# Two accumulators per bank or one: the PSUM placement of a seven-product matrix stage

## The chip, the cores and the metric

The kernel runs on one core of one Trainium2 chip. The metric is the device time of one execution in microseconds (us), lower being better. Before the change it is 1694.95 us, the median of three runs (1694.61 to 1696.0).

## What is computed

A two-layer encoder trunk over 512 tokens of width 1024. Each layer adds a mixer of three attention branches to its input, then a feed-forward block. The change touches one product inside the second of these, the down projection:

```python
def conv_ffn(h, w_up, conv_w, conv_b, w_down):        # h: (1, 512, 1024)
    u = h @ w_up                                      # w_up: (1024, 5632)
    u = depthwise_conv3(u, conv_w) + conv_b
    a, g = jnp.split(u, 2, axis=-1)
    return (jax.nn.gelu(g) * a) @ w_down              # w_down: (2816, 1024)

for l in range(2):
    x = x + mixer(rmsnorm(x, norm1_g[l]))
    x = x + conv_ffn(rmsnorm(x, norm2_g[l]), w_up[l], conv_w[l], conv_b[l], w_down[l])
```

All of it is float32, and the kernel keeps more precision than one float32r pass of TensorE has: every operand is split into a high part (rounded to float32r) and a low part (the rest), and a product is three matmuls, high by high, high by low and low by high.

## The kernel before

**Layout.** Activations lie transposed: `self.x[k]` is block k of 128 features by 512 tokens, k from 0 to 7. A weight block of 128 by 128 is the stationary operand, and 512 (or 256) token columns move past it. PSUM has eight banks of 512 float32 columns per partition, and `bank("d")` hands them out in turn, here as a ring of eight.

**The seven-product stage.** Of the 22 blocks of 128 hidden features, the first 12 go through a Strassen-like scheme instead of a plain product. The tokens are cut in two halves of 256, the hidden blocks into even and odd ones, and the output blocks are taken in pairs (m, m+1), for m = 0, 2, 4, 6. For such a pair, which this text calls a unit, eight block products are replaced by seven products of sums, each of 6 stationary blocks with 3 matmuls, so 18 matmuls of 256 columns. A stage has 4 units, 28 products and 504 matmuls, and there is one stage per layer, placed among the up projections as soon as the first 12 hidden blocks are there; up projections (`("up", f)`, matmuls of 512 columns) stand before and after it.

The moving operands (the tiles `ft`, columns B11, T1, B21, T2, B22, T4, T3) are made once, in `sum_operands`. The stationary operands are sums of the down weights, made per unit by `prepare_sum` (L165 to L180): four pieces come by DMA (tiles `own` and `raw`), VectorE adds them up to S1 (L169), S3 (L173), S2 (L174) and S4 (L177), and `split` (L192 and L193) makes of each a high part `whi` on ScalarE and then a low part `wlo` on VectorE. There are three buffers for a `whi` and `wlo` pair, so the pair for product j+3 can be written once product j has been multiplied.

**The accumulators.** In a unit the products, numbered j = 0 to 6, go into PSUM regions that are summed further where the scheme wants running sums. After every product VectorE adds the region, or subtracts it, into a half of `x[m]` or `x[m+1]` (L1010, 256 columns; for j = 6 into both halves, L1013). This read is called an eviction below. The region isn't cleared afterwards: a later product in the same region adds to what stands there, and is read out again. Before the change the four regions are the two halves of two banks:

- bank 0, first half: j = 0, 3 and 6; second half: j = 2
- bank 1, first half: j = 1 and 4; second half: j = 5

The first matmul into a bank carries the start flag (`start=j < 2 and i == 0`). [...]

**Order.** PE and the DMA queue of SP run in the order of the code. ScalarE and VectorE are ordered by a list scheduler, in which evictions have a higher priority (`high_priority(offset=EVAC)`). The framework puts the semaphore waits in, and it treats a bank as one thing: a matmul into a bank waits until VectorE's earlier reads of that bank are over, whichever half they read.

Of the kernel before, what the change touches and what calls it, by code (L numbers as in the profile page):

```python
# [41 lines left out]
B11, B21, B22, T1, T3, T2, T4 = range(7)  # L42
# [20 lines left out]
class Trunk:  # L63
# [926 lines left out]
    def do_sum(self, m):  # L990


        nc, mm = self.nc, self.nc.tensor.matmul
        banks = [self.bank("d") for _ in range(2)]
        first, second = slice(0, 256), slice(256, 512)
        x1, x2 = self.x[m], self.x[m + 1]
        steps = ((B11, 0, first, x1[:, first], 1), (T1, 1, first, x2[:, second], -1), (B21, 0, second, x1[:, first], 1),
                 (T2, 0, first, x1[:, second], 1), (B22, 1, first, x1[:, second], 1), (T4, 1, second, x2[:, first], -1),
                 (T3, 0, first, x2, -1))
        for j, (spec, (operand, b, part, x, sign)) in enumerate(zip(self.W["sum", m], steps)):  # L1000
            ps = banks[b][:, part]
            c = slice(operand * 256, operand * 256 + 256)
            for i, (wh, wl) in enumerate(self.weights(spec)):
                hi, lo = (t[:, c] for t in self.ff[i])
                mm(ps, wh, hi, start=j < 2 and i == 0, stop=False, skip_group_check=True)  # L1005
                mm(ps, wh, lo, start=False, stop=False, skip_group_check=True)  # L1006
                mm(ps, wl, hi, start=False, stop=i == NP - 1, skip_group_check=True)  # L1007
            with self.tc.high_priority(offset=EVAC):
                if j < 6:
                    nc.vector.tensor_tensor(x, x, ps, ALU.add if sign > 0 else ALU.subtract)  # L1010
                else:
                    both = x.rearrange("p (n c) -> p n c", c=256)
                    nc.vector.tensor_tensor(both, both, ps.rearrange("p (n c) -> p n c", n=1).to_broadcast([P, 2, 256]),  # L1013
                                            ALU.subtract)
        if m == KD - 2:
            self.ff = self.ff[NP:]
            self.fas.close()
            self.fbs, self.fb = self.open("fb")
# [202 lines left out]
```

## Time and profile before

| What | Value |
|---|---|
| Three timed runs | 1694.95 us median, 1694.61 to 1696.0 |
| The profiled execution, its own time | 1695.11 us |
| Its span in the profile | 1693.3 us |
| Instructions | 23333 |
| TensorE (PE) busy | 1673.5 us, 99% |
| Weight loads (PEld), beside PE | 1402.3 us, 83% |
| VectorE (DVE) busy | 1216.9 us, 72% |
| ScalarE (ACT) busy | 867.7 us, 51% |
| DMA engines, mean | 92 GB/s |

How to read the profile: busy time counts each engine's instructions in one profiled execution. A PE row in the timeline has its start, its modelled length, and in brackets the idle time before it with the instruction that ended this. Matmuls overlap: one of 256 columns is shown 0.28 us long, and the next begins well before it ends. So PE's pace is read from the distance between starts, not from lengths. Where a row waited for several semaphores, the profile names the one it takes to have come last.

### The profile page before, as it was taken

The page shows a single profiled execution, that of the slowest core. Times are in us where ns is not written, and L with a number is a line of the kernel's source. Part 1 is how long each engine was busy: PE and PEld are TensorE (multiplying, and loading weights), DVE is VectorE, ACT ScalarE, POOL GpSimd, SP SyncE. Part 2 cuts the span into 40 slices and gives each one's busy share as a digit, 9 for nine tenths or more (in the row PEclk, how much of TensorE's full clock was granted, in tenths as well). Part 3 has the DMA queues.
Part 4 walks back from the last instruction along what each step waited for, and adds up shares of the span by engine and source line. Part 5 has one row for each costly group of instructions (what it writes and reads, how often), then busy time and mean ns, then how long its engine had stood idle before and what let it go on. Part 6 is the DMA issues. An engine that isn't in the chain of part 4 may idle for free.

```text
span 1693.3 us, 23333 instructions
## 1 busy us (share of the span) xinstructions
PE 1673.5 (99%) x8898; PEld 1402.3 (83%) x8898; DVE 1216.9 (72%) x2033; ACT 867.7 (51%) x1525; POOL 52.1 (3%) x107
## 2 busy tenths in 40 slices
PE   9999999999999999999999999999999999999998
PEld 8888888888888888888887888888888888888887
DVE  7677866787559897676567687767866598876755
ACT  7664445775435443344466554567744454433443
POOL 1110000000000000000011100000000000000000
PEclk9999999999999999999999999999999999999999
DMA  6233323222333333432232323332233333323322
GB/s 181 71 97 91 88 79 88 77 65 80 111 87 112 99 83 92 125 99 76 83 96 81 96 77 93 82 87 69 63 87 105 103 111 101 90 73 113 93 81 88
DMA packets 289664, 155.53 MB, mean 92 GB/s; under 512 B 9136, under 2 KB 285632, under 8 KB 289552
## 3 DMA queue, kind: packets, MB, share of 16 engines
q1 hardware_dynamic: 287008, 148.88, 30.9%
q0 software_dynamic: 2256, 4.83, 0.9%
q8 instruction: 70, 1.15, 0.3%
q14 instruction: 42, 0.34, 0.1%
q10 hardware_dynamic: 288, 0.33, 0.1%
HBM read 151.89 MB, written 2.10 MB: 91 GB/s over the span
## 4 chain that ended last, share of the span: by engine, by line
PE 94%; DVE 4%; ACT 1%; issue 0%; DMA 0%; ACTq 0%
PE ps_ring L206 12%; PE ps_ring L207 12%; PE ps_ring L208 12%; PE ps_d L208 10%; PE ps_d L206 10%; PE ps_d L207 10%; PE ps_g L206 4%; PE ps_g L208 4%; PE ps_g L207 4%; PE ps_d L1005 2%; PE ps_d L1006 2%; PE ps_d L1007 2%; PE ps_ring L286 2%; PE ps_ring L273 1%; DVE wlo L193 1%; PE ps_g L306 1%
## 5 line engine op out<-in xcount | busy, mean ns | idle before, releaser
L192 ACT CAST whi<-raw 128x1024 fp32r<-128x1024 f32 (+3 forms) x347 | 297.3, 857 | 508.6 <-PE ps_ring L207 152.5
L193 DVE TENSOR_TENSOR wlo<-raw,whi 128x1024 fp32r<-128x1024 f32 (+4 forms) x345 | 339.2, 983 | 83.2 <-ACT whi L192 82.5
L208 PE MATMUL ps_d<-hh,wlo 128*128 128x512 f32 x685 | 266.6, 389 | 0.0
L207 PE MATMUL ps_d<-hl,whi 128*128 128x512 f32 x685 | 266.5, 389 | 0.0
L206 PE MATMUL ps_d<-hh,whi 128*128 128x512 f32 x685 | 266.5, 389 | 0.0
L206 PE MATMUL ps_ring<-hh,whi 128*128 128x512 f32 x600 | 235.3, 392 | 0.5 <-DVE pt L717 0.5
L208 PE MATMUL ps_ring<-hh,wlo 128*128 128x512 f32 x600 | 233.7, 390 | 0.0
L207 PE MATMUL ps_ring<-hl,whi 128*128 128x512 f32 x600 | 233.6, 389 | 0.0
L208 PEld LDWEIGHTS ps_d<-hh,wlo 128*128 128x128 f32 x685 | 128.6, 188 | 27.1 <-DVE wlo L193 0.2
L207 PEld LDWEIGHTS ps_d<-hl,whi 128*128 128x128 f32 x685 | 128.6, 188 | 26.9
L206 PEld LDWEIGHTS ps_d<-hh,whi 128*128 128x128 f32 x685 | 128.6, 188 | 26.3
L206 PEld LDWEIGHTS ps_ring<-hh,whi 128*128 128x128 f32 x600 | 112.6, 188 | 24.5 <-DVE pt L717 0.9
L208 PEld LDWEIGHTS ps_ring<-hh,wlo 128*128 128x128 f32 x600 | 112.6, 188 | 23.7
L207 PEld LDWEIGHTS ps_ring<-hl,whi 128*128 128x128 f32 x600 | 112.7, 188 | 23.0
L1005 PE MATMUL ps_d<-ft,whi 128*128 128x256 f32 x336 | 96.4, 287 | 10.9 <-DVE x L1010 8.1
L1006 PE MATMUL ps_d<-ft,whi 128*128 128x256 f32 x336 | 95.0, 283 | 0.0
L1007 PE MATMUL ps_d<-ft,wlo 128*128 128x256 f32 x336 | 94.9, 283 | 0.0
L199 DVE TENSOR_TENSOR u<-ps_d,rb 128x512 f32<-128x512 f32 x80 | 55.1, 689 | 54.3 <-PE ps_d L208 54.0
L199 DVE TENSOR_TENSOR gz<-ps_ring,rb 128x512 f32<-128x512 f32 x44 | 30.4, 691 | 78.0 <-PE ps_ring L208 78.0
L1005 PEld LDWEIGHTS ps_d<-ft,whi 128*128 128x128 f32 x336 | 64.2, 191 | 14.1 <-issue 9.0
L193 DVE TENSOR_TENSOR pl<-ps_ring,ph 128x512 fp32r<-128x512 f32 x104 | 65.6, 682 | 1.6 <-ACT ph L192 1.6
L1006 PEld LDWEIGHTS ps_d<-ft,whi 128*128 128x128 f32 x336 | 64.4, 192 | 0.1
(355 smaller groups left out, 3262.9 us busy)
## 6 DMA issues: line engine op xcount, KB each, us to landing
raw<-in_w_in_dram SPq DMA_DIRECT2D x86, 512.0 KB, 3.9
raw<-in_w_up_dram SPq DMA_DIRECT2D x80, 512.0 KB, 3.8
raw<-in_w_down_dram SPq DMA_DIRECT2D x32, 384.0 KB, 3.6
own<-in_w_down_dram SPq DMA_DIRECT2D x16, 384.0 KB, 4.9
raw<-in_w_in_dram SPq DMA_DIRECT2D x17, 256.0 KB, 3.0
raw<-in_w_br_mla_dram SPq DMA_DIRECT2D x16, 256.0 KB, 2.8
raw<-in_w_br_na_dram SPq DMA_DIRECT2D x16, 256.0 KB, 2.9
raw<-in_w_br_gqa_dram SPq DMA_DIRECT2D x16, 256.0 KB, 2.9
```

Source lines behind the costliest of these rows:

```text
L192: nc.scalar.copy(hi, src)
L193: nc.vector.tensor_sub(lo, src, r32(hi))
L199: self.nc.vector.tensor_tensor(out, a, b, ALU.mult)
L206: mm(ps, sh, mh, start=first and k == 0, stop=False)
L207: mm(ps, sh, ml, start=False, stop=False)
L208: mm(ps, sl, mh, start=False, stop=last and k == n - 1)
L273: self.nc.tensor.transpose(out[i][:, n * 64:n * 64 + 64], block[q], self.idf[q, q])
L286: self.nc.tensor.matmul(out, st[a], mv[b], start=first and t == 0, stop=last and t == 2)
L306: self.nc.tensor.matmul(self.gbank[j], w[:, j * P:(j + 1) * P], m, start=n + t == 0, stop=False)
L1005: mm(ps, wh, hi, start=j < 2 and i == 0, stop=False, skip_group_check=True)
L1006: mm(ps, wh, lo, start=False, stop=False, skip_group_check=True)
L1007: mm(ps, wl, hi, start=False, stop=i == NP - 1, skip_group_check=True)
```

## The change

Each unit takes four banks in place of two, and uses the first 256 columns of each. B11, T2 and T3 (j = 0, 3, 6) stay together in the first, T1 and B22 (j = 1, 4) in the second; B21 (j = 2) has the third for itself and T4 (j = 5) the fourth. Four matmuls per unit carry the start flag in place of two. The number of matmuls, their operands and the evictions' arithmetic are the same. A stage takes 16 turns of the ring of eight in place of 8, so the banks that are handed out after it are the same as before.

```diff
-        banks = [self.bank("d") for _ in range(2)]
+        banks = [self.bank("d")[:, :256] for _ in range(4)]
...
-        steps = ((B11, 0, first, x1[:, first], 1), (T1, 1, first, x2[:, second], -1), (B21, 0, second, x1[:, first], 1),
-                 (T2, 0, first, x1[:, second], 1), (B22, 1, first, x1[:, second], 1), (T4, 1, second, x2[:, first], -1),
-                 (T3, 0, first, x2, -1))
-        for j, (spec, (operand, b, part, x, sign)) in enumerate(zip(self.W["sum", m], steps)):
-            ps = banks[b][:, part]
+        steps = ((B11, 0, x1[:, first], 1), (T1, 1, x2[:, second], -1), (B21, 2, x1[:, first], 1),
+                 (T2, 0, x1[:, second], 1), (B22, 1, x1[:, second], 1), (T4, 3, x2[:, first], -1), (T3, 0, x2, -1))
+        for j, (spec, (operand, b, x, sign)) in enumerate(zip(self.W["sum", m], steps)):
+            ps, fresh = banks[b], j in (0, 1, 2, 5)
...
-                mm(ps, wh, hi, start=j < 2 and i == 0, stop=False, skip_group_check=True)
+                mm(ps, wh, hi, start=fresh and i == 0, stop=False, skip_group_check=True)
```

The function is one line shorter, so L1005, L1006, L1007, L1010 and L1013 of before are L1004, L1005, L1006, L1009 and L1012 of the changed kernel.

The first place is on PE, in the first unit of the first stage, where j = 2 (B21) ends and j = 3 (T2) begins; `ps_d` is the accumulator's bank tile, and a bracket names the engines whose semaphores the row waits for. Before:

```order
L1005 MATMUL ps_d_6083<-ft_5903,whi_6085 128x256
L1006 MATMUL ps_d_6083<-ft_5904,whi_6085 128x256
L1007 MATMUL ps_d_6083<-ft_5903,wlo_6086 128x256
L1005 MATMUL ps_d_6083<-ft_5089,whi_6115 128x256 [waits DVE_49,Activation_49]
L1006 MATMUL ps_d_6083<-ft_5090,whi_6115 128x256
L1007 MATMUL ps_d_6083<-ft_5089,wlo_6116 128x256
```

And in the changed kernel:

```order
L1004 MATMUL ps_d_6085<-ft_5903,whi_6087 128x256
L1005 MATMUL ps_d_6085<-ft_5904,whi_6087 128x256
L1006 MATMUL ps_d_6085<-ft_5903,wlo_6088 128x256
L1004 MATMUL ps_d_6083<-ft_5089,whi_6117 128x256 [waits DVE_49,Activation_49]
L1005 MATMUL ps_d_6083<-ft_5090,whi_6117 128x256
L1006 MATMUL ps_d_6083<-ft_5089,wlo_6118 128x256 [waits DVE_49]
```

Nothing moved, but the tiles differ: before, j = 2 and j = 3 write the same bank tile (6083); now j = 2 has a tile of its own (6085), and j = 3 goes back to the tile of j = 0.

The second place is on PE too, in the same unit, where j = 4 (B22) ends and j = 5 (T4) begins. Before:

```order
L1005 MATMUL ps_d_6084<-ft_5903,whi_6138 128x256
L1006 MATMUL ps_d_6084<-ft_5904,whi_6138 128x256
L1007 MATMUL ps_d_6084<-ft_5903,wlo_6139 128x256
L1005 MATMUL ps_d_6084<-ft_5089,whi_6161 128x256 [waits DVE_49,Activation_49]
L1006 MATMUL ps_d_6084<-ft_5090,whi_6161 128x256
L1007 MATMUL ps_d_6084<-ft_5089,wlo_6162 128x256
```

And in the changed kernel:

```order
L1004 MATMUL ps_d_6084<-ft_5903,whi_6140 128x256
L1005 MATMUL ps_d_6084<-ft_5904,whi_6140 128x256
L1006 MATMUL ps_d_6084<-ft_5903,wlo_6141 128x256
L1004 MATMUL ps_d_6086<-ft_5089,whi_6163 128x256 [waits Activation_49]
L1005 MATMUL ps_d_6086<-ft_5090,whi_6163 128x256
L1006 MATMUL ps_d_6086<-ft_5089,wlo_6164 128x256 [waits DVE_49]
```

The first matmul of j = 5 has a new tile and no longer waits for VectorE; the third, which reads `wlo`, does. In all, the double wait (VectorE and ScalarE) stands on j = 2, 3 and 5 of a unit before, and on j = 3, 4 and 6 now, 24 of them in two stages either way.

The third place is on VectorE, in the second unit of the first stage; `x2_69` and `x3_70` are the outputs into which its evictions add, `wlo` rows are low parts of weights, L169, L173 and L177 the weight sums. Before, from the eviction of the unit ahead (j = 6) on:

```order
L169 TENSOR_TENSOR s1_6385<-raw_6287,own_6289 128x768 [waits DMAHW5_49,DMAHW4_49,DVE_49]
L1013 TENSOR_TENSOR x1_68<-x1_68,ps_d_6083 128x512 [waits PE_49]
L193 TENSOR_TENSOR wlo_6262<-raw_6234,whi_6261 128x768 [waits DMAHW2_49,Activation_49]
L173 TENSOR_TENSOR raw_6287<-own_6285,raw_6287 128x768 [waits DMAHW3_49,DVE_49]
L1010 TENSOR_TENSOR x2_69<-x2_69,ps_d_6259 128x256 [waits PE_49]
L177 TENSOR_TENSOR raw_6234<-own_6109,raw_6234 128x768 [waits DVE_49]
L193 TENSOR_TENSOR wlo_6292<-own_6109,whi_6291 128x768 [waits Activation_49]
L1010 TENSOR_TENSOR x3_70<-x3_70,ps_d_6260 128x256 [waits PE_49]
L193 TENSOR_TENSOR wlo_6315<-raw_6234,whi_6314 128x768 [waits Activation_49]
L1010 TENSOR_TENSOR x2_69<-x2_69,ps_d_6259 128x256 [waits PE_49]
L193 TENSOR_TENSOR wlo_6338<-own_6113,whi_6337 128x768 [waits Activation_49]
```

And in the changed kernel:

```order
L1012 TENSOR_TENSOR x1_68<-x1_68,ps_d_6083 128x512 [waits DVE_49,PE_49]
L169 TENSOR_TENSOR s1_6389<-raw_6291,own_6293 128x768 [waits DMAHW5_49,DMAHW4_49,DVE_49]
L193 TENSOR_TENSOR wlo_6266<-raw_6236,whi_6265 128x768 [waits DMAHW2_49,Activation_49]
L1009 TENSOR_TENSOR x2_69<-x2_69,ps_d_6261 128x256 [waits PE_49]
L173 TENSOR_TENSOR raw_6291<-own_6289,raw_6291 128x768 [waits DMAHW3_49,DVE_49]
L193 TENSOR_TENSOR wlo_6296<-own_6111,whi_6295 128x768 [waits Activation_49]
L177 TENSOR_TENSOR raw_6236<-own_6111,raw_6236 128x768 [waits DVE_49]
L1009 TENSOR_TENSOR x3_70<-x3_70,ps_d_6262 128x256 [waits PE_49]
L1009 TENSOR_TENSOR x2_69<-x2_69,ps_d_6263 128x256 [waits DVE_49,PE_49]
L193 TENSOR_TENSOR wlo_6319<-raw_6236,whi_6318 128x768 [waits Activation_49]
L193 TENSOR_TENSOR wlo_6342<-own_6115,whi_6341 128x768 [waits Activation_49]
```

The weight sum L169, which waits for a DMA, now stands behind the eviction of j = 6; the eviction of j = 2 (the second `x2_69` row) now stands ahead of the low part for j = 4 (`wlo_6319`), and was behind it. Outside the stages VectorE, ScalarE, PE and SP keep their order.

## The prediction

> **What bounds the kernel now.** I read the page first, then PE's waits, then the timeline of PE and VectorE through one stage. Of the page:
>
> ```profile
> span 1693.3 us, 23333 instructions
> PE 1673.5 (99%) x8898; PEld 1402.3 (83%) x8898; DVE 1216.9 (72%) x2033; ACT 867.7 (51%) x1525; POOL 52.1 (3%) x107
> PE 94%; DVE 4%; ACT 1%; issue 0%; DMA 0%; ACTq 0%
> L1005 PE MATMUL ps_d<-ft,whi 128*128 128x256 f32 x336 | 96.4, 287 | 10.9 <-DVE x L1010 8.1
> ```
>
> PE is the bound, and the chain that ends last runs through it for 94%. So only what shortens PE's own stream, or its gaps, counts. The last row is the one big gap on the page: before the first kind of seven-product matmul PE stands idle for 10.9 us. PE's waits, longest first in total, say for whom:
>
> ```profile
> PE ps_d L1005 <- DVE x L1010: 8.1, 13, 0.7
> PE ps_d L1005 <- ACT whi L192: 2.6, 3, 0.9
> ```
>
> Sixteen waits: two in each of the eight units. The timeline of the third unit of the first stage shows both kinds (columns: start, length, engine and line; in brackets the idle time ahead and what ended it).
>
> ```profile
> 653.75 0.28 PE L1006 MATMUL ps_d<-ft,whi 128*128 128x256 f32 x1
> ...
> 664.30 0.28 PE L1007 MATMUL ps_d<-ft,wlo 128*128 128x256 f32 x1
> 665.18 0.36 PE L1005 MATMUL ps_d<-ft,whi 128*128 128x256 f32 x1 [0.61 <-DVE x L1010]
> 665.37 0.28 PE L1006 MATMUL ps_d<-ft,whi 128*128 128x256 f32 x1
> ...
> 670.34 0.36 PE L1005 MATMUL ps_d<-ft,whi 128*128 128x256 f32 x1 [0.61 <-DVE x L1010]
> ```
>
> ```profile
> 664.61 0.42 DVE L1010 TENSOR_TENSOR x<-x,ps_d 128x256 f32<-128x256 f32 x1 [0.18 <-PE ps_d L1007]
> ```
>
> The first is the start of j = 3, the second of j = 5. Each goes into the bank that the product just ended has filled the other half of (j = 2, j = 4). So PE ends at 664.30 + 0.28 = 664.58, VectorE reads from 664.61 to 665.03, and PE goes on 0.15 later, at 665.18. The loss isn't the 0.61 of the bracket. Between gaps matmuls start (664.30 - 653.75) / 88 = 0.1199 apart (88 steps between those two rows). The gap is 0.88 from start to start, so 0.76 is lost, and another 0.07 at the second matmul (0.19 in place of 0.12): 0.83 per wait.
>
> The three waits put down to ScalarE are of the same kind, with VectorE late. In the second unit:
>
> ```profile
> 646.97 0.95 DVE L193 TENSOR_TENSOR wlo<-raw,whi 128x768 fp32r<-128x768 f32 x1
> 647.84 0.42 DVE L1010 TENSOR_TENSOR x<-x,ps_d 128x256 f32<-128x256 f32 x1
> ```
>
> ```profile
> 648.40 0.35 PE L1005 MATMUL ps_d<-ft,whi 128*128 128x256 f32 x1 [0.89 <-ACT whi L192]
> ```
>
> The row of PE comes 0.14 after the eviction's end (647.84 + 0.42), as above; the eviction had a low part of weights ahead of it (one such takes VectorE 0.87 until the next can start).
>
> **The size of it.** I don't add up sixteen rows, but take the length of the two stages, from the first matmul of 256 columns to the first up projection behind:
>
> ```profile
> 623.82 0.28 PE L1005 MATMUL ps_d<-ft,whi 128*128 128x256 f32 x1
> ...
> 691.50 0.40 PE L206 MATMUL ps_d<-hh,whi 128*128 128x512 f32 x1
> ```
>
> ```profile
> 1461.73 0.28 PE L1005 MATMUL ps_d<-ft,whi 128*128 128x256 f32 x1
> ...
> 1530.02 0.40 PE L206 MATMUL ps_d<-hh,whi 128*128 128x512 f32 x1
> ```
>
> 67.68 and 68.29 us; 504 matmuls at 0.1199 are 60.43. So 7.25 + 7.86 = 15.1 us are lost in the two stages. That is the most that taking every wait out can give. Sixteen times 0.83 is 13.3; the rest is the late evictions and three short waits at j = 2.
>
> **The change, part by part.**
>
> *The waits at j = 3 and j = 5.* The order's rows show j = 5 going into a bank of its own without a wait for VectorE ahead of its first matmul, and j = 3 returning to the bank of j = 0, two products earlier. The same holds for j = 4 (bank of j = 1) and j = 6 (bank of j = 3). Two products are 36 × 0.1199 = 4.3 us for an eviction that needs 0.03 + 0.42 + 0.15 = 0.6, so it may queue 3.7 us on VectorE before PE notices. The short waits at j = 2 go as well. Term: -15.1.
>
> *The double waits.* There are 24 of them as before, now all on evictions long over. What one costs then, the row of j = 2 in the second unit shows, whose eviction had ended 0.2 earlier:
>
> ```profile
> 645.20 0.29 PE L1005 MATMUL ps_d<-ft,whi 128*128 128x256 f32 x1
> 645.33 0.28 PE L1006 MATMUL ps_d<-ft,whi 128*128 128x256 f32 x1
> ```
>
> 0.13 to the next in place of 0.12. Term: 24 × 0.01 = +0.24; between nothing and 0.07 each (1.7), the restart after a real wait.
>
> *Start flags.* Two more per unit on matmuls that run anyway: the rows of 623.82 (with) and 653.75 (without) are alike, 0.28. Nothing; the sum goes unchanged with it.
>
> *What is late next.* Weights. In the first unit of each stage VectorE is still busy with the convolution:
>
> ```profile
> 631.71 0.95 DVE L193 TENSOR_TENSOR wlo<-raw,whi 128x768 fp32r<-128x768 f32 x1
> ```
>
> ```profile
> 628.22 0.36 PE L1005 MATMUL ps_d<-ft,whi 128*128 128x256 f32 x1
> ```
>
> That `wlo` is for j = 4 and its queue ahead is unchanged, so it ends at 632.66, and PE can use it 0.15 later, at 632.81. Undelayed, j = 2 starts at 628.13 (the row's 628.22 less its wait of 0.09), and the third matmul of j = 4 is 38 steps on, at 632.69. So about 0.12 + 0.07 = 0.2 stays, once per stage: +0.4.
>
> In the second unit VectorE now evicts j = 2 before it makes the low part for j = 4, and its queue is held up first by a DMA. The worst case is in the second stage:
>
> ```profile
> 1473.78 0.54 SPq L163 DMA_DIRECT2D own<-in_w_down_dram  x1
> ```
>
> ```profile
> 641.36 0.96 DVE L169 TENSOR_TENSOR s<-raw,own 128x768 f32<-128x768 f32 x1 [0.68 <-DMA own<-in_w_down_dram]
> ...
> 1471.36 0.70 DVE L199 TENSOR_TENSOR c<-c 128x512 f32<-128x512 f32 x1
> ...
> 1479.61 0.96 DVE L169 TENSOR_TENSOR s<-raw,own 128x768 f32<-128x768 f32 x1 [1.01 <-DMA own<-in_w_down_dram]
> ```
>
> ```profile
> 664.54 0.83 ACT L192 CAST whi<-own 128x768 fp32r<-128x768 f32 x1 [1.23 <-PE ps_d L1006]
> ```
>
> The sum (last VectorE row) waited for a DMA that was issued 5.8 us earlier, and SP had issued that once a low part on VectorE, for j = 6 of the unit ahead, had freed a buffer. In the changed order this low part no longer has L199 in front of it, 0.7, so the sum starts at about 1478.9. The unit starts on PE at 1461.73 + 126 × 0.1199 + 0.2 = 1477.0, so the sum comes 1.9 us into it. Behind it stand in turn a low part (0.87), an eviction (0.4), a sum (0.87), the low part for j = 3, which ends at about 5.8 and is needed at 56 × 0.1199 = 6.7; then a sum until 6.7, two evictions, the second of which can't start before j = 2 is over (6.6), until 7.3; meanwhile the high part of j = 4 on ScalarE, 0.83, until 7.6; and its low part until 8.6. PE needs that at 74 × 0.1199 = 8.87, less 0.15. It fits by 0.1; in the first stage, where the same sum came 17.54 after the stage's start (641.36) and not 17.88, by 0.4. I take zero, with 0.5 for the range. VectorE as a whole has room:
>
> ```profile
> 641.00:691.60 50.60, 37.11 (x51) 1.00 0.28 80
> ```
>
> 37.11 us of work in three units, where the shorter stage leaves 3 × 15.1 = 45.3.
>
> *The sum.* -15.1 + 0.24 + 0.4 = -14.5 us. Nothing behind the stage takes it back: the up projections that follow have their banks in the same turn, and PE runs through them without idle time. The span of 1693.3 becomes 1678.8, the profiled execution's own 1695.11 becomes 1680.6, and the median of 1694.95, which is 0.16 lower, 1680.5.
>
> **The clock, and a rule for the pace.** PE's granted clock through the stages, and ahead of them (window, its length, busy time and count of PE, PEld, DVE, ACT and POOL, then the clock, DMA share and GB/s):
>
> ```profile
> 580.00:623.80 43.80, 43.80 (x195) 36.27 (x194) 37.46 (x54) 19.93 (x28) 0.00 (x0) 1.00 0.37 102
> 623.80:691.50 67.70, 62.44 (x505) 60.92 (x504) 52.85 (x76) 26.05 (x32) 0.72 (x1) 1.00 0.30 83
> ```
>
> Full clock with gaps and without. The pace of 0.1199 for 256 columns could itself come from two accumulators sharing a bank. The up projections, with whole banks, tell against it:
>
> ```profile
> 619.74 0.39 PE L206 MATMUL ps_d<-hh,whi 128*128 128x512 f32 x1
> ...
> 623.59 0.39 PE L208 MATMUL ps_d<-hh,wlo 128*128 128x512 f32 x1
> ```
>
> 17 steps in 3.85 us are 0.2265 for 512 columns, so 0.1066 for each 256 columns more, and 0.013 per matmul whatever its length. The overhead is there in whole banks too, so the pace stays. [...]
>
> **Rivals.**
>
> *Weights take over* (0.12). VectorE or the DMA is later than walked through, and PE waits for `wlo` where it waited for the bank. For it: margins of 0.1 to 0.4 in four units. Against: 3 us of slack per unit. At 0.5 to 1.5 us in each of the eight units 4 to 12 of the 14.5 are lost; likelier the low end: 1682.5 to 1688.
>
> *Half of it* (0.03). The rows give the engine that j = 3 waits for, not which instruction of it. Were it still the eviction just ahead, only the waits at j = 5 would go, 8 × 0.83 = 6.6: 1688.3. The bank tile speaks against it.
>
> *Nothing* (0.03). Every bank wait turns into a weight wait of its length: 1695.
>
> *The pace* (0.01). The share of the bank does slow the matmuls; by the difference at 512 columns no more than 0.013 each, 1008 × 0.013 = 13 us more: 1667.5.
>
> *Slower* (0.03). [...]
>
> **How the numbers follow.** My forecast, 0.78, is 1680.5, its own range 1679.3 (all 15.1, and 0.5 for the spread of the runs) to 1683 (the double waits at 0.07, the 0.5 of the margins, and the spread again). For 8 in 10 the range goes on into the first rival's near half: 1679 to 1685. About 0.2% (3.4 us) is what a measurement of this kernel tells from no change. Faster by more: 0.78 + 0.12 + 0.03 + 0.01 = 0.94; within: 0.03; slower: 0.03.
>
> **What would show it.** The stages should take about 60.7 us each, PE's idle time ahead of the first matmul line of the stage should fall from 10.9 us to under 1, and the waits for the eviction should leave PE's list. VectorE's evictions then end later relative to PE without anybody waiting. A new row in which PE waits for `wlo` (L193), of 0.1 to 0.2 us once per stage, is expected; such rows in every unit would be the first rival. [...] If the stages shrink by 14 us and the whole doesn't, I was wrong about what stands behind them.

## The result and the profile after

| | Before | After |
|---|---|---|
| Median | 1695.18 us (four runs, 1694.61 to 1696.0) | 1682.05 us (four runs, 1681.14 to 1682.36) |
| Ratio, with its 95% interval | | 0.9921 [0.9904, 0.9938] |
| Profiled execution: own time, span | 1695.11, 1693.3 us | 1681.14, 1679.3 us |
| First stage, from its first matmul to the first up projection behind | 67.68 us | 60.92 us |
| Second stage | 68.29 us | 61.47 us |

The change makes the kernel 13.1 us faster (a fourth run of the kernel before has moved its median from 1694.95 to 1695.18). The forecast was 1680.5, and the range reached from 1679 to 1685. The last two rows of the table come from these rows of PE's timeline after the change:

```profile
623.24 0.28 PE L1004 MATMUL ps_d<-ft,whi 128*128 128x256 f32 x1
...
684.16 0.40 PE L206 MATMUL ps_d<-hh,whi 128*128 128x512 f32 x1
...
1454.56 0.28 PE L1004 MATMUL ps_d<-ft,whi 128*128 128x256 f32 x1
...
1516.03 0.40 PE L206 MATMUL ps_d<-hh,whi 128*128 128x512 f32 x1
```

The stages are 6.76 and 6.82 us shorter, 13.6 in all. The stretch between them is the same (770.40 us, 770.23 before), and so is the one behind them (1679.3 - 1516.03 = 163.27, and 1693.3 - 1530.02 = 163.28 before): what was gained in a stage was kept. The remaining 0.4 of the 14.0 between the two spans comes from the stretch ahead of the first stage, which began at 623.24 in place of 623.82; the change touches nothing there. Runs of one kernel differ by that much: in a second profile of the changed kernel the first stage begins at 623.72.

The page after the change, in the lines that answer to those of before:

```profile
span 1679.3 us, 23339 instructions
PE 1669.9 (99%) x8898; PEld 1400.5 (83%) x8898; DVE 1214.5 (72%) x2033; ACT 866.9 (52%) x1525; POOL 52.6 (3%) x107
L1006 PE MATMUL ps_d<-ft,wlo 128*128 128x256 f32 x336 | 95.6, 284 | 0.5 <-DVE wlo L193 0.4
L1004 PE MATMUL ps_d<-ft,whi 128*128 128x256 f32 x336 | 95.1, 283 | 0.0
```

PE's idle time ahead of the first of the three matmul lines fell from 10.9 us to 0.0. In its place the third one, which reads the low part of the weights, shows 0.5. In the list of PE's waits the eviction (L1009) doesn't stand any more, and the one row on the stage is:

```profile
PE ps_d L1006 <- DVE wlo L193: 0.4, 1, 0.4
```

What an eviction does now can be seen where j = 4 ends in the third unit of the first stage. VectorE reads the bank from 664.92 on, while PE goes on with j = 5 in another bank at its pace of 0.12:

```profile
664.92 0.42 DVE L1009 TENSOR_TENSOR x<-x,ps_d 128x256 f32<-128x256 f32 x1 [0.45 <-PE ps_d L1006]
```

```profile
664.96 0.28 PE L1006 MATMUL ps_d<-ft,wlo 128*128 128x256 f32 x1
665.08 0.28 PE L1004 MATMUL ps_d<-ft,whi 128*128 128x256 f32 x1
```

**What is left.** 504 matmuls at 0.1199 are 60.43 us, so 0.5 and 1.0 us are still lost. The largest single loss is in the second stage, at j = 3 of the third unit:

```profile
1491.74 0.28 PE L1005 MATMUL ps_d<-ft,whi 128*128 128x256 f32 x1
1492.41 0.39 PE L1006 MATMUL ps_d<-ft,wlo 128*128 128x256 f32 x1 [0.40 <-DVE wlo L193]
1492.63 0.28 PE L1004 MATMUL ps_d<-ft,whi 128*128 128x256 f32 x1
```

0.67 and 0.22 from start to start in place of 0.12 each: 0.65 lost. VectorE's queue shows why the low part for j = 3 is late (the `wlo` row of 1491.40 is that low part):

```profile
1487.59 0.96 DVE L169 TENSOR_TENSOR s<-raw,own 128x768 f32<-128x768 f32 x1 [1.56 <-DMA own<-in_w_down_dram]
1488.47 0.95 DVE L193 TENSOR_TENSOR wlo<-raw,whi 128x768 fp32r<-128x768 f32 x1
1489.34 0.95 DVE L173 TENSOR_TENSOR raw<-own,raw 128x768 f32<-128x768 f32 x1
1490.20 0.41 DVE L1009 TENSOR_TENSOR x<-x,ps_d 128x256 f32<-128x256 f32 x1
1490.54 0.95 DVE L177 TENSOR_TENSOR raw<-own,raw 128x768 f32<-128x768 f32 x1
1491.40 0.95 DVE L193 TENSOR_TENSOR wlo<-own,whi 128x768 fp32r<-128x768 f32 x1
```

VectorE stood 1.56 us for a DMA, ahead of a weight sum (S1, L169) that serves the next unit and is in no hurry. From then on its queue runs without a gap until the low part ends at 1492.35, and PE starts 0.06 later. SP had issued that DMA at

```profile
1481.26 1.54 SPq L163 DMA_DIRECT2D own<-in_w_down_dram  x1
```

6.3 us earlier. Smaller losses of the same kind are 0.33 in the third unit of the first stage and 0.22 in the second unit of the second; 0.13 per stage at j = 4 of the first unit has another cause, VectorE's convolution work: there its queue runs without a gap up to the low part for j = 4 (631.13 to 632.08 in the first stage), with L951 and L952, 0.74 us each, at 629.15 and 630.47, and PE starts 0.06 after the low part, at 632.14.

### The profile page after: what moved, and what is told of

It is laid out like the page before. It is cut to its first block, busy times and chain, and to the rows that moved or that the text cites. A ratio compares the mean times of both kernels' runs of the same rounds, so it can differ in the third digit from the quotient of the medians.

```text
span 1679.3 us, 23339 instructions
## 1 busy us (share of the span) xinstructions
PE 1669.9 (99%) x8898; PEld 1400.5 (83%) x8898; DVE 1214.5 (72%) x2033; ACT 866.9 (52%) x1525; POOL 52.6 (3%) x107
## 4 chain that ended last, share of the span: by engine, by line
PE 93%; DVE 4%; DMA 1%; ACT 1%; issue 0%; SPq 0%; DVEq 0%; ACTq 0%
PE ps_ring L206 13%; PE ps_ring L207 12%; PE ps_ring L208 12%; PE ps_d L208 11%; PE ps_d L206 11%; PE ps_d L207 11%; PE ps_g L208 4%; PE ps_g L206 4%; PE ps_g L207 4%; PE ps_ring L286 2%; DVE wlo L193 2%; PE ps_d L1006 1%; PE ps_d L1005 1%; PE ps_d L1004 1%; PE ps_ring L273 1%; DMA own<-in_w_down_dram 1%
## 5 line engine op out<-in xcount | busy, mean ns | idle before, releaser
L1006 PE MATMUL ps_d<-ft,wlo 128*128 128x256 f32 x336 | 95.6, 284 | 0.5 <-DVE wlo L193 0.4
L1004 PE MATMUL ps_d<-ft,whi 128*128 128x256 f32 x336 | 95.1, 283 | 0.0
L1005 PE MATMUL ps_d<-ft,whi 128*128 128x256 f32 x336 | 95.1, 283 | 0.0
L1006 PEld LDWEIGHTS ps_d<-ft,wlo 128*128 128x128 f32 x336 | 64.5, 192 | 1.2 <-DVE wlo L193 1.0
L1004 PEld LDWEIGHTS ps_d<-ft,whi 128*128 128x128 f32 x336 | 64.5, 192 | 0.1
```

Source lines behind the costliest of these rows:

```text
L1004: mm(ps, wh, hi, start=fresh and i == 0, stop=False, skip_group_check=True)
```

## The experiments

Theory A: what the change removed is the wait of a product for the eviction from the bank that its predecessor has just filled, one wait per such pair of neighbours, and nothing else about banks matters. What is left after it is VectorE's wait for the DMA ahead of S1. The rivals stand in the expectations. Ten kernels ran, each beside the kernel before on the same chip, and a gain is counted against the median of the kernel before measured there: 1695.55 for the two halves of the change, S1 on GpSimd and the fourth buffer; 1694.89 for the last two runs; 1695.00 for the others. "Stages" is the length of both, taken as in the table above: 135.97 before, 122.39 after. It comes from one profiled execution of each kernel, which need not be the median one.

**The changed kernel again**, unaltered.

> The changed kernel once more, unaltered, as the base for the others on this chip. Every theory: faster than the kernel before by 13 to 14 us, about 1682, the two stages 60.9 and 61.5 us long, with one wait of PE for a low part of weights in the third unit of the second stage.

1682.03 us, ratio 0.9925 [0.9912, 0.9937]; stages 61.14 + 61.73 = 122.87. Two profiles of one kernel thus differ by 0.5 in the stages: the same waits stand at the same places, 0.8 in place of 0.65 at the largest, and two of 0.1 join them. This profile is of the median execution, the one above of the fastest of its four.

**Two full banks, products swapped.** Nothing of the change itself is in this kernel. Every bank still holds two accumulators, and the start flags are as before.

```diff
-ORDER = ("V11", "S1", "V12", "S2", "S4", "V22", "S3")
+ORDER = ("V11", "S1", "V12", "S4", "S2", "V22", "S3")
...
-                 (T2, 0, first, x1[:, second], 1), (B22, 1, first, x1[:, second], 1), (T4, 1, second, x2[:, first], -1),
+                 (B22, 1, first, x1[:, second], 1), (T2, 0, first, x1[:, second], 1), (T4, 1, second, x2[:, first], -1),
```

> The two full banks of before, but products j = 3 (T2) and j = 4 (B22) change places, so that the banks alternate and no product goes into the bank that the one just ahead has filled. Theory A (the loss was the wait for an eviction from the bank just filled, and nothing else about the banks): both waits of each unit go, 13 to 15 us, 1680 to 1682, with 60.5 to 61.5 us per stage, though every bank still holds two accumulators. Rival B (half-used banks are what helps, be it the start flag or the share of a bank): no gain, 1694 to 1696. Rival C (one product, 2.16 us, is too short a cover for an eviction that queues on VectorE): part of the gain, short waits left at j = 2 to 6, 1684 to 1690.

1683.36 us, ratio 0.9931 [0.9919, 0.9944]. Its stages are 62.79 and 62.22. On PE's timeline the largest loss in the first is:

```profile
630.93 0.39 PE L1007 MATMUL ps_d<-ft,wlo 128*128 128x256 f32 x1 [0.68 <-DVE wlo L193]
```

And PE's waits:

```profile
PE ps_d L1007 <- DVE wlo L193: 1.3, 2, 0.7
...
PE ps_d L1005 <- DVE x L1010: 0.2, 1, 0.2
```

11.0 of the 13.6 us in the stages come back with two banks. Rival B falls: neither half-used banks nor start flags are what helps. The time lies 1.4 above theory A's band and 0.6 below rival C's, and the rows say why it isn't quite the changed kernel: of the 4.15 us that the two stages still lose, 3.15 stand at j = 3, at a wait for the low part of S4, which the swap needs one product sooner, and not for an eviction. The largest are the 0.93 in the first unit of each stage (the row of 630.93 and its follower). Rival C is right in a small part: 0.90 stands at j = 2, whose eviction has one product of cover, and more than half of it in the third unit of the first stage (0.48), where the eviction stood behind S1's DMA.

**Half of the change: B21 alone.**

```diff
-        banks = [self.bank("d")[:, :256] for _ in range(4)]
+        full = [self.bank("d") for _ in range(4)]
+        banks = [full[0][:, :256], full[1][:, :256], full[2][:, :256], full[1][:, 256:]]
...
-            ps, fresh = banks[b], j in (0, 1, 2, 5)
+            ps, fresh = banks[b], j in (0, 1, 2)
```

> One half of the change: B21 (j = 2) has a bank of its own, T4 (j = 5) stays in the second half of the bank of T1 and B22. Theory A (each wait belongs to one pair of neighbours in one bank): the waits at j = 3 and the short ones at j = 2 go, the eight at j = 5 stay at 0.83 us each, so the stages are about 64 us each and the time is 7 to 8 us under the kernel before, 1687 to 1688. Rival (one of the two waits covers the other, so that taking one out only moves the loss to the other, or to the weights): 0 to 4 us, 1691 to 1695.

1688.96 us, ratio 0.9962 [0.995, 0.9975], 6.6 us less than before. Its waits:

```profile
PE ps_d L1005 <- DVE x L1010: 5.5, 8, 0.9
```

The time misses theory A's band by 1.0. The first stage is as expected (64.24), the second isn't (65.54): low parts are late there, 0.78 and 0.53 at j = 3 of the second and third unit.

**The other half: T4 alone**, the same with T4 in a bank of its own and B21 in `full[0][:, 256:]`.

> The other half: T4 (j = 5) has a bank of its own, B21 (j = 2) stays in the second half of the bank of B11, T2 and T3. Theory A: the waits at j = 5 go, those at j = 3 and the short ones at j = 2 stay, the stages are about 64.3 us each, 6.5 to 7 us less in all, 1688 to 1689; and the gains of the two halves add up to a little more than the whole change's 13, since late weights show less while waits are left. Rival: 0 to 4 us, or 13 already.

1688.67 us, ratio 0.9964 [0.9951, 0.9976], 6.9 us less. Its waits:

```profile
PE ps_d L1005 <- DVE x L1010: 4.4, 8, 0.7
PE ps_d L1005 <- ACT whi L192: 2.6, 3, 0.9
```

Each half takes out its own eight waits and leaves the other eight (5.5 us in 8 waits at j = 5 in the first; in the second 8 at j = 3, three of them under ScalarE's name, as before, and three at j = 2 under VectorE's). By the medians the gain is nearly linear in the number of pairs: 13.5 for the two halves together, 13.1 for the whole, as expected. In the profiled executions, though, the halves give 6.2 and 5.2 us in the stages (129.78 and 130.81), 11.4 where the whole gives 13.6. The profiled execution of the T4 kernel was the slowest of its five (1690.22, 1.5 above its median; stages 65.20 and 65.61), and its rows show most of the difference: in its second unit j = 2 now waits for the eviction of j = 0, two products back.

```profile
644.64 0.36 PE L1005 MATMUL ps_d<-ft,whi 128*128 128x256 f32 x1 [0.60 <-DVE x L1010]
```

```profile
641.47 0.96 DVE L169 TENSOR_TENSOR s<-raw,own 128x768 f32<-128x768 f32 x1 [1.02 <-DMA own<-in_w_down_dram]
642.35 0.95 DVE L193 TENSOR_TENSOR wlo<-raw,whi 128x768 fp32r<-128x768 f32 x1
643.22 0.95 DVE L173 TENSOR_TENSOR raw<-own,raw 128x768 f32<-128x768 f32 x1
644.08 0.41 DVE L1010 TENSOR_TENSOR x<-x,ps_d 128x256 f32<-128x256 f32 x1
```

The same 1.0 us for the DMA, with the eviction third in the queue behind it. So PE, where it is faster, meets S1's DMA in whatever its layout makes it wait for.

**What is left, first try: another order of the DMAs.**

```diff
-        for name in {0: ("V11", "V21", "V22"), 2: ("V12",)}.get(j, ()):
+        for name in {0: ("V11", "V22", "V21"), 2: ("V12",)}.get(j, ()):
```

> The changed kernel, with the DMA of the weight piece V22 issued ahead of that of V21, so that the pair that the sum S1 waits for lands earlier. Theory A for what was left of the waits (VectorE stands 1.0 to 1.6 us for that DMA in the second and third unit, and its queue behind is late by that): the idle time ahead of S1 falls to under 0.5 us, the waits of PE at j = 3 of the third unit and j = 4 of the second go, the stages are 60.6 us each, 1.2 us less in all, about 1680.9. Rival (the low part for j = 4 behind the eviction of j = 2, or VectorE being too full, is the cause): the waits of PE stay, 1682.

1681.95 us, ratio 0.9924 [0.9911, 0.9938]; stages 60.60 + 61.60 = 122.20. The first stage lost its waits as expected, the second kept them (0.77 at j = 3 of the third unit). The line on what VectorE stood idle for ahead of S1, and the times to landing of the weight pieces:

```profile
  DMA raw<-in_w_down_dram: 5.5, 6
...
DMA to landing us min/median/max: 3.5/5.6/6.7
```

The expectation failed: over the whole run the idle time isn't less (5.4 us in 5 waits after the change), it only has the other piece's name. V21 now lands last. Unit by unit, though, the rows speak for theory A. In the second and third units VectorE works through the same order of instructions in this kernel and in both profiles of the changed one; what differs is how long S1 waited for its DMA. In us, that wait, and behind the stroke what PE then loses in that unit:

| | First stage, unit 2 | unit 3 | Second stage, unit 2 | unit 3 |
|---|---|---|---|---|
| Changed kernel | 1.02 / 0 | 1.24 / 0.33 | 1.36 / 0.22 | 1.56 / 0.65 |
| The same again | 1.28 / 0.13 | 1.33 / 0.42 | 1.39 / 0.24 | 1.80 / 0.89 |
| V22 first | 0.88 / 0 | 0.74 / 0 | 1.39 / 0.25 | 1.67 / 0.76 |

In these three profiles waits of 1.02 us and less cost PE nothing, and longer ones cost it more, the longer they are in the same unit. Were the order of the queue or a VectorE that is too full the cause by itself, the first stage of this kernel would have kept its losses.

**The same DMA order with two banks**, both edits together.

> Both of the two runs above: two full banks, j = 3 and 4 swapped, and V22's DMA ahead of V21's. Theory A: as the changed kernel with the earlier DMA, 1680.5 to 1682. Rival B: 1694 to 1696. Rival C: 1683 to 1689.

1682.98 us, ratio 0.9929 [0.9917, 0.9942]; stages 61.66 + 61.66. The time lies 1.0 above theory A's band, just under rival C's. Inside these stages S1 doesn't wait for its DMA any more (with the swap alone it waited 0.28, 0.66 and 0.22 us), no eviction was waited for beyond 0.2, and the late low parts at j = 3 of the second and third units cost 0.06 or less in place of 0.3; the first unit's 0.93 is the loss that stays.

**What is left, second try: S1 on GpSimd.**

```diff
-            add(unit["S1"], unit["V21"], unit["V22"])
+            self.nc.gpsimd.tensor_tensor(unit["S1"], unit["V21"], unit["V22"], ALU.add)
```

> The changed kernel with the weight sum S1 on GpSimd, which has nothing else to do in the stages, so that VectorE's queue no longer stands behind its DMA. Theory A for what is left: VectorE never waits for that DMA, PE's waits at j = 4 of the second and j = 3 of the third unit go, whatever the DMA takes, only 0.13 us at j = 4 of the first unit stays; stages of 60.6 us, about 1681. Rival 1 (the eviction of j = 2 ahead of the low part for j = 4 is the cause): the wait in the second unit stays. Rival 2 (GpSimd working beside VectorE slows VectorE's instructions): rows of VectorE longer than 0.95 us during S1, and a wait somewhere else, 1682 or more.

1683.44 us, ratio 0.9928 [0.9915, 0.994]; stages 61.36 + 61.64 = 123.00. In the third units the waits at j = 3 shrink to 0.04 or less, as theory A has it, but 0.24 is lost at j = 3 of the second unit of the second stage, and the first units lose 0.9 us each, at j = 2 and 3:

```profile
621.23 2.22 POOL L169 TENSOR_TENSOR s<-raw,own 128x768 f32<-128x768 f32 x1 [14.10 <-DVE wlo L193]
```

```profile
621.67 2.06 DVE L986 SCALAR_TENSOR_TENSOR tt<-tt,prod 128x256 f32<-128x256 f32 x1
...
657.29 2.49 DVE L177 TENSOR_TENSOR raw<-own,raw 128x768 f32<-128x768 f32 x1
```

```profile
631.71 0.38 PE L1006 MATMUL ps_d<-ft,wlo 128*128 128x256 f32 x1 [0.31 <-DVE wlo L193]
```

GpSimd takes 2.0 us (mean of eight) for what takes VectorE 0.96, and rival 2 came true. Six VectorE rows began while GpSimd was at S1, and all six became longer: L986, 0.41 in the changed kernel, took 2.06 ahead of the first unit of either stage, and L177, 0.95 there, took 2.1 to 2.6 in the second and third units. Each ended 0.3 to 0.8 after GpSimd's row; what they waited for on the way isn't shown. The other rows of these two lines kept their 0.41 and 0.95. So VectorE was still held up by S1, only through GpSimd, and this run is no clean test of theory A.

**What is left, third try: a fourth buffer for raw pieces.**

```diff
-                t = self.wp.tile([P, 1024], F32, tag="raw", name="raw", bufs=RAWB)
+                t = self.wp.tile([P, 1024], F32, tag="raw", name="raw", bufs=RAWB + 1)
```

(and the same in `load`, which uses the same buffers)

> The changed kernel with a fourth buffer for raw weight pieces, so that V21's DMA, which waits for a buffer, and V22's behind it in SP's queue can start up to 1.6 us earlier. Theory A for what is left (S1 waits for these two at the head of VectorE's queue): the idle time ahead of S1 falls from 1.0 to 1.6 us to under 0.4, and PE's waits at j = 4 of the second and j = 3 of the third unit go: stages of 60.6 us, 1.0 to 1.3 us less than the changed kernel, about 1681. Rival (the two transfers share the DMA engines, and land no earlier): idle time and waits stay, 1682.

1679.7 us, ratio 0.9909 [0.9894, 0.9924]; stages 60.58 and 60.60:

```profile
623.10 0.28 PE L1004 MATMUL ps_d<-ft,whi 128*128 128x256 f32 x1
...
683.68 0.40 PE L206 MATMUL ps_d<-hh,whi 128*128 128x512 f32 x1
...
1453.94 0.28 PE L1004 MATMUL ps_d<-ft,whi 128*128 128x256 f32 x1
...
1514.54 0.40 PE L206 MATMUL ps_d<-hh,whi 128*128 128x512 f32 x1
```

The waits at j = 3 and 4 of the second and third unit are gone, the eviction of j = 2 still stands ahead of the low part for j = 4, and only the first unit's 0.13 is left. So that position in the queue costs nothing by itself, and together with the table above this makes S1's DMA the cause of the rest. VectorE still stood 2.2 us for it in two places, both ahead of the stages. This is the fastest version, 15.9 us under the kernel before; about 1 of these lies outside the stages, where the buffer serves other loads too, and no run shows what it comes from. Against the changed kernel the stages are 1.2 us shorter (1.7 against its second profile); the two intervals overlap, and the two kernels weren't measured beside each other.

**The fourth buffer without the change.** This asks whether the late DMA was there before.

> The kernel before, with the fourth raw buffer alone. Theory A (the late DMA of the weight pieces was hidden behind the bank waits before, and the change laid it bare): all sixteen bank waits stay, only the short wait of 0.34 us at j = 2 of the second unit of the second stage goes, so 0 to 0.6 us less, 1694.5 to 1695.5. Rival (the buffer helps by itself, elsewhere or in the stages): 2 us or more less, as it did on top of the change, 1693 or under.

1693.32 us, ratio 0.999 [0.998, 0.9999], 1.6 less; stages 67.40 and 67.41:

```profile
624.22 0.28 PE L1005 MATMUL ps_d<-ft,whi 128*128 128x256 f32 x1
...
691.62 0.40 PE L206 MATMUL ps_d<-hh,whi 128*128 128x512 f32 x1
...
1461.89 0.28 PE L1005 MATMUL ps_d<-ft,whi 128*128 128x256 f32 x1
...
1529.30 0.40 PE L206 MATMUL ps_d<-hh,whi 128*128 128x512 f32 x1
```

```profile
PE ps_d L1005 <- DVE x L1010: 9.9, 16, 0.7
```

The sixteen waits stay, now all under VectorE's name and none over 0.7. But the stages are 1.2 us shorter, twice what theory A allowed, and the time lies between the two bands. The DMA was not hidden behind the bank waits before: it made the evictions late, and PE paid for it there (the three waits of 0.9 under ScalarE's name, and the short one at j = 2). So my statement that the change laid it bare was wrong. The DMA cost 1.2 us before and about as much after, in another place.

**The fourth buffer with two banks.**

> The two full banks with j = 3 and j = 4 swapped, and the fourth raw buffer. Theory A: with the late DMA gone, only the first unit's waits stay (0.16 at j = 2 and 0.93 at j = 3, where the low part of S4 is late), so 61.6 us per stage, 1681.5 to 1682; two banks come within 2 us of four. Rival (two banks leave evictions too little cover once nothing else delays PE): waits for evictions in every unit, 1683 or more.

1682.03 us, ratio 0.9927 [0.9913, 0.9941]; stages 61.66 + 62.14. As theory A has it, but for 0.5 more in the second unit of the second stage, where S1 waited 0.39 us for its DMA after all. By the medians two banks come within 2.3 us of four, not within 2.

## Why the prediction was right

**The mechanism, and its size.** The two runs with the fourth buffer are the clean comparison, free of the DMA: 134.81 us with sixteen waits, 121.18 without, 13.6 less. The rows add up to that: twelve waits of 0.83 and the four in first units, of 0.89, are 13.5; two of the three short waits at j = 2, 0.15 each, make it 13.8; and the first units give back 0.12 each at j = 4. The prediction's price of 0.83, read in a third unit, is a little low for first units only. The two halves of the change and the swapped order confirm that the price belongs to the pair of neighbours in one bank. With the waits at j = 3 gone as well as those at j = 5, the rival "half of it" falls.

**The term that was mis-sized.** The changed kernel gained 13.6 in the stages, where the sum said 14.5. Every wait for an eviction went, as the first term (-15.1) has it. But 1.5 us came back as waits for low parts, where the sum had 0.4 for the first units and zero for the others: 0.25 in the first units, and 1.2 in the second and third. The prediction had noticed that 15.1 is more than 13.3, and put the rest down to "the late evictions and three short waits at j = 2", which "go as well". Of that rest 1.2 us weren't a matter of banks: VectorE was late, and it stayed late, now with a low part that PE waits for.

**The walk through VectorE's queue** named the right cause, the DMA ahead of S1, and the right kind of wait, but its result "It fits by 0.1; I take zero" failed. In the unit that it walked through, the second of the second stage, S1 began 2.2 us into the unit (1472.04, the unit having begun at 1469.80) and not 1.9, and 0.22 was lost at j = 4. And it took the second unit for the worst case. The third unit was worse, for two reasons. S1 began 2.5 us into it (1487.59, the unit having begun at 1485.1), since the DMA took 6.3 us and not 5.8. And VectorE makes the sum S4 (L177) there ahead of the low part for j = 3, as the rows of 1490.54 and 1491.40 show, while in the second unit it makes them the other way round (the last order listed under "The change"). By the walk's own figures that sum moves the end of the low part from 5.8 to 6.7 us, which is when PE needs it. The margin there was too small, and the range, not the forecast, held the 1.2 us.

**How close it was.** The median, 1682.05, lies nearer to the low end of the first rival, *weights take over* (1682.5), than to the forecast of 1680.5. That rival came true in part: PE waits for `wlo` in three of the six units behind the first ones, 0.22 to 0.65 us each, where the rival had 0.5 to 1.5 in all eight units. That the profiled execution, 1681.14, is within 0.6 of its forecast of 1680.6 is partly luck, as it was the fastest of the four.

**The double waits** were priced at 0.24. After the change the stages show no excess at them beyond 0.03 each, and with the fourth buffer 121.18 less the first units' 0.25 is 120.93, against 120.86 for 1008 matmuls at 0.1199: 0.07 for all 24, hardly more than the rounding of the pace leaves open (0.05). **The first unit's wait** was forecast at 0.2 per stage and is 0.13: PE starts 0.06 after the end of a low part (1492.35 to 1492.41 above), where the prediction had 0.15.

**The other rivals.** The pace between waits is 0.12 as before, so sharing a bank didn't slow the matmuls. *Slower* falls with the median, and no run's granted clock, as its mean, is under 0.999. In the profiled execution it is 1.00 in both stages, with PE busy for 60.83 of 60.90 us in the first (columns as in the prediction):

```profile
623.20:684.10 60.90, 60.83 (x505) 60.52 (x505) 51.77 (x76) 25.79 (x32) 0.66 (x1) 1.00 0.33 88
1454.50:1516.00 61.50, 61.10 (x505) 60.62 (x505) 51.82 (x76) 25.78 (x32) 0.00 (x0) 1.00 0.32 87
```

## What to carry to other kernels

Where one engine fills an accumulator while another empties its neighbour, ask which earlier read each first write has to wait for, and how many products lie between. Here no product between cost 0.83 us or more each time, one product was nearly enough (0.90 us at j = 2 in the two stages of the swapped order), two were enough (after the change no eviction is waited for), and changing the order of the products did most of what more banks did (11.0 of 13.6 us). When waits are counted by subtraction, the part that exceeds count times price may be a second cause, as 1.2 of 1.8 us were here, and such a cause can stay when the first is removed.

## What the runs showed that I had not expected

The time from issue to landing of the same weight pieces differs from kernel to kernel: median 4.6 us and at most 5.7 before, 4.9 and 6.2 after, 5.6 and 6.7 with V22 ahead of V21, 4.2 and 5.7 with a fourth buffer, but 4.8 and 6.9 with that buffer and two banks. It may go with how closely they are issued; no run isolates that. One issue on SP, usually 0.54 us, took up to 1.62 before and 1.54 after. In the changed kernel issuing a piece earlier in the queue didn't make the pair land in time in the second stage; a free buffer did.

Giving a VectorE sum to an idle GpSimd wasn't free for VectorE: its own rows that began beside it took up to 2.6 us in place of 0.95.
